# Second feed-forward with four chunk pairs whose weight sums are made in DRAM

## The chip, the cores and the metric

The kernel runs on one core of a Trainium2 chip. The metric is the device time of one execution in microseconds (us); lower is better. A profiled execution also gives a span, from the first to the last instruction of the program, which leaves out what lies around it. Engines are called as the profile calls them: PE (TensorE, matrix multiply), PEld (its weight loads), DVE (VectorE), ACT (ScalarE), POOL (GpSimd) and SP (SyncE, which here only issues transfers).

## The reference, cut to what matters

One layer of an encoder block on 256 positions with 1024 features, all in 32-bit floats:

```python
h = rmsnorm(x, ffn1_pre_g);  x = x + 0.5 * rmsnorm(swiglu(h, ffn1_w_in, ffn1_w_down), ffn1_post_g)
#  mixer: a gated linear recurrence and a forgetting attention on one projection of x, merged by gates
#  cross attention to 256 memory positions
h = rmsnorm(x, ffn2_pre_g);  x = x + 0.5 * rmsnorm(swiglu(h, ffn2_w_in, ffn2_w_down), ffn2_post_g)

def swiglu(h, w_in, w_down):
    gate, up = jnp.split(h @ w_in, 2, axis=-1)      # w_in: 1024 x 5632
    return (jax.nn.silu(gate) * up) @ w_down        # w_down: 2816 x 1024
```

The change is in how the last line of the layer, the second feed-forward, gets `h @ w_in`.

## The kernel before

**Units.** Every weight matrix lies in DRAM as units of 128 x 1024 floats (512 KB). `load_split` (L134) loads one unit into a tile `raw` by a transfer that SP issues (L143), ACT copies it, rounded, to `hi` (L145) and DVE subtracts to get `lo` (L147). Products of two such split operands take three matmuls: hi·hi, hi·lo and lo·hi. There are four `raw` buffers and eight `hi` and eight `lo` buffers. A `raw` buffer is free again when L147 has read it, a `hi`/`lo` pair when its last matmul has. Each call appends its transfer to the list `loads`, and SP issues in that order.

**The feed-forward.** `ffn` (L418) cuts the 2816 hidden columns into 11 chunks of 256. A chunk's weights are four units of `w_in` (two halves of the 1024 inputs by gate and up columns side by side); its share of `w_down` is two units. In the second feed-forward chunks 0 and 1 are done row-wise (`act_tok`), chunks 2, 3, 4, 5 and 8 column-wise (`act_col`, L453), each with 32 matmuls of 512 columns and 32 of 256. `down` (L486) takes a finished chunk through its two units of `w_down`, 12 matmuls of 512 columns for each half of the positions.

**Pairs.** Chunks 6 and 7, and 9 and 10, are done together (`act_pair`, L548), in both feed-forwards (`PAIRS`, L36). The 2 x 2 block product of the two halves of x (positions by inputs) with the two chunks' weights (inputs by chunks) is done with seven block products in place of eight, each of 12 matmuls of 512 columns. For that, four differences of blocks of x are formed once (`pair_inputs`, L506, after chunk 2), and sums of weight blocks are formed for each pair: W00+W01, W01+W11, W00+W01+W11 and the sum of all four. DVE adds them in SBUF (L573) in tiles `sraw` of four further buffers (tag `extra`), so that a pair loads eight units, splits fourteen pairs of tiles and adds eight times. Its activations come out by rows and need eight 128 x 128 transposes (`flush`, L427). Between two block products `step_between` puts one half of a `down`, 12 matmuls.

**Order of the work.** The program is written as one stream; a scheduler orders each engine's instructions by that stream, except where `after(n)` or `issue_after` ties them to a certain matmul or transfer. `row_of` (L348) turns the column of row factors into a row by two small transfers on POOL's queue through DRAM; `act_col` and `pair_inputs` need that row. After the last pair the `down` of chunk 7 follows, and then those of chunks 8 to 10, cut by output columns.

Of the kernel before, what the change touches and what calls it, by code (L numbers as in the profile page):

```python
# [18 lines left out]
P = 128  # L19
D = 1024  # L20
# [12 lines left out]

STAG = 3

PAIRS = {"f1_in": (6, 9), "f2_in": (6, 9)}  # L36

L_ACT = 21
L_F1 = 24
# [41 lines left out]
def block_kernel(ctx: ExitStack, tc: tile.TileContext, wts, head_in, gf_in, x_in, mem_in, memT_in, cols, rows, fbias, masks, out):  # L81
# [48 lines left out]

    place = {}

    def parts_of():
        return [wp.tile([P, D], F32R, tag=t, name=nm(t), bufs=8) for t in ("hi", "lo")]  # L134

    def load_split(src, n=512, behind=None, parts=None):

        raw = wp.tile([P, D], F32, tag="raw", name=nm("raw"), bufs=4)
        hi, lo = parts or parts_of()
        r, h, l = raw, hi, lo  # L140
        if n < 512:
            r, h, l = (p.rearrange("p (k n) -> p k n", k=2)[:, :, :n] for p in (raw, hi, lo))
        loads.append(nc.sync.dma_start(r, src).ins)  # L143
        with tc.issue_after(behind[0]) if behind else nullcontext():
            S.copy(h, r)  # L145
        with tc.issue_after(behind[1]) if behind else nullcontext():
            V.tensor_tensor(out=l, in0=r, in1=h.bitcast(F32), op=ALU.subtract)  # L147
        return hi, lo
# [270 lines left out]
    def ffn(w_in, w_dn, X, r2, n_tok, i_row, first_half, second_half=None):  # L419
# [83 lines left out]

        def pair_inputs():  # L506
            rho = sp.tile([P, P], F32, tag="c1", name=nm("rho"), bufs=7)
# [3 lines left out]
            V.reciprocal(q, r2[1])  # L511
            V.tensor_tensor(out=q, in0=r2[0], in1=q, op=ALU.mult)
            xf = [m4([P, 4, T], n="xf") for _ in range(2)]
            for k in range(2):
                for i in range(2):
                    x = X.t[2 * k + i].bitcast(F32)
                    V.tensor_tensor(out=xf[k][:, 2 * i : 2 * i + 2], in0=x[:, :, 0], in1=x[:, :, 1], op=ALU.add)
                V.tensor_tensor(out=xf[k][:, :, P:], in0=xf[k][:, :, P:], in1=bc(rho, [P, 4, P], 1), op=ALU.mult)
            a, b, d, e = (xf[k][:, :, h * P : h * P + P] for h in range(2) for k in range(2))
            ss = [m4([P, 2, 4, P], n="ss") for _ in range(2)]  # L520
            de, aed, ad, baed = (t[:, i] for t in ss for i in range(2))
            V.tensor_tensor(out=de, in0=d, in1=e, op=ALU.subtract)
            V.tensor_tensor(out=aed, in0=a, in1=de, op=ALU.subtract)
            V.tensor_tensor(out=ad, in0=a, in1=d, op=ALU.subtract)
            V.tensor_tensor(out=baed, in0=b, in1=aed, op=ALU.subtract)
            out = {}
            for n, x in (("baed", baed), ("aed", aed), ("de", de), ("ad", ad), ("e", e)):
                t = m4([P, 2, 4, P], F32R, "sx")
                split(t[:, 0], t[:, 1], x)
                out[n] = t  # L530
            return out, q

        def sum_load(c, n, halves):
            t = []
            for j in range(2):
                r = wp.tile([P, D], F32, tag="extra", name=nm("sraw"), bufs=4)
                more(r, c, *halves[0], j, None)
                t.append(r)
            return t

        def more(r, c, k, n, j, op):
            src = wts[_AT[w_in] + 4 * (c + n) + 2 * k + j - 4]
            if op is None:
                loads.append(nc.sync.dma_start(r, src).ins)
            else:
                G.dma_start(r, src, accum_op=op)

        def act_pair(c, between):  # L548
            sx, q = pairs_in
# [4 lines left out]
            def of_x(k):  # L554
                return lambda kk: (X.hi(4 * k + kk, 0, P), X.lo(4 * k + kk, 0, P))

            def splits(t):
                u = []
                for r in t:
                    p = parts_of()  # L560
                    split(p[0], p[1], r)
                    u.append(p)
                return u

            def raws(k, n):
                t = [wp.tile([P, D], F32, tag="raw", name=nm("raw"), bufs=4) for _ in range(2)]
                for j in range(2):
                    more(t[j], c, k, n, j, None)
                return t

            def add(t, o):
# [14 lines left out]
            def half_tile(n):  # L586
                return sp.tile([P, 512], F32, tag="z2", name=nm(n), bufs=3)

            sums, both = sums_of_pair.pop(c)
# [4 lines left out]
            product(b0, of_x(0), splits(sums), True)  # L594
            S.copy(p1, b0)
            step_between()
# [5 lines left out]
            add(sums, both)  # L602
            add(both, raw)
            b3 = trp()
            product(b3, of("de"), splits(sums), True)
            add(sums, raw)
            step_between()
            b1 = trp()
            product(b1, of("aed"), splits(sums), True)
# [8 lines left out]
            add(sums, raw)  # L618
            step_between()
            b4 = mm()  # L620
            product(b4, of("ad"), splits(both), True)
# [8 lines left out]
            product(b4, of("e"), splits(sums), False)  # L630
            with tc.high_priority():
                t = half_tile("c10")
                V.tensor_tensor(out=t, in0=v, in1=b4, op=ALU.add)
# [4 lines left out]
                step_between()  # L638

        def pair_loads(c):  # L640
            if c in pairs and c not in sums_of_pair:
                with tc.issue_after(loads[-1]):
                    sums_of_pair[c] = sum_load(c, 0, ((0, 0), (0, 1))), sum_load(c, 1, ((0, 1), (1, 1)))

        sums_of_pair = {}
        pairs, pairs_in = PAIRS[w_in], None
        for c in range(n_tok):
            acts[c] = m4([P, 2, 2, T], F32R, "act")
        for h in range(2):
            m = len(log)  # L650
            for c in range(n_tok):
                act_tok(c, h)
            if h == 0 and n_tok:
                second_half(m)
                row = row_of(fac[3])
        accs = None
        done = 0
        if callable(r2):
# [8 lines left out]
        for c in range(n_tok, NFF):  # L667
            if c - 1 in pairs:
                continue
            if c in pairs:  # L670
                pair_loads(c)
            acts[c] = m4([P, 2, 2, T], F32R, "act")
            if c in pairs:
                acts[c + 1] = m4([P, 2, 2, T], F32R, "act")
                downs = [(i, h) for i in range(done, min(c, NFF - STAG - 1)) for h in range(2)]
                done = max(done, min(c, NFF - STAG - 1))
# [7 lines left out]
                act_pair(c, [lambda i=i, h=h: one(i, h) for i, h in downs])  # L684
            elif c == 2 and first_half:
                n = len(log)
                (outs,) = act_first((c,), mm)
                for h in range(2):
                    flush(n + L_ACT + 24 * h)
                    act_evac(outs[h], c, h)  # L690
            else:
# [16 lines left out]
            if c == 2 and pairs:  # L708
# [29 lines left out]

    X1 = Joined()
    heads, raw1 = [], []
    for kb in range(KB):
# [813 lines left out]
```

## Time and profile before

| What | Value |
|---|---|
| median of 3 runs | 776.87 us (776.84 to 778.01) |
| the profiled execution itself | 776.83 us |
| its span | 774.6 us |
| granted PE clock over the span | 0.998 |
| bytes moved by DMA | 148.08 MB, 191 GB/s on the mean |
| transfers of whole units on SP's queue | 231 into `raw`, 16 into `sraw` |

The span is 2.2 us shorter than the execution's own time. Busy times are shares of the span. Matmuls are pipelined, and the length the profile gives one is not the time until the next can start, so in what follows the time of a group of matmuls is read from one start to another.

### The profile page before, as it was taken

To read this page: it belongs to the slowest core of one execution; us is meant where nothing else is said; L and a number is where in the kernel's file an instruction comes from. 1 tells how busy PE (TensorE), PEld (TensorE's weight loads), DVE (VectorE), ACT (ScalarE), POOL (GpSimd) and SP (SyncE) were. 2 spreads that over 40 slices of the span, in tenths; PEclk is the share of its full clock that TensorE was granted. 3 is DMA by queue.
4 is the path that set the end of the run, shared out by engine and by line. 5 is a ranking of instruction groups with operands and counts; after the bars stand their busy time and mean duration, and the time that the engine had idled before them with its cause. 6 is when DMAs were issued, how large, how long until landed. Compare 5 with 4: busy or idle time off the path is not lost.

```text
span 774.6 us, 11943 instructions
## 1 busy us (share of the span) xinstructions
PE 766.7 (99%) x4454; PEld 654.9 (85%) x4454; DVE 636.3 (82%) x989; ACT 489.5 (63%) x807; POOL 15.8 (2%) x39
## 2 busy tenths in 40 slices
PE   9999999999999999999999999999999999999996
PEld 7888888888888998898888888889888888888875
DVE  6797999998778899888776665885579698999993
ACT  7666565768765678557676345863668556565762
POOL 0000000000000101100000000000000000000000
PEclk9999999999999999999999999999999999999999
DMA  9749477255744545834676654465175637467241
GB/s 340 266 140 303 160 260 274 101 194 195 228 160 146 180 144 183 281 110 176 203 265 229 216 176 159 156 201 207 39 247 179 195 119 260 166 226 289 82 136 55
DMA packets 44507, 148.08 MB, mean 191 GB/s; under 512 B 5145, under 2 KB 8865, under 8 KB 44449
## 3 DMA queue, kind: packets, MB, share of 16 engines
q1 hardware_dynamic: 43168, 144.83, 54.3%
q0 software_dynamic: 848, 2.12, 1.1%
q8 instruction: 35, 0.57, 0.3%
q10 hardware_dynamic: 432, 0.37, 0.1%
q14 instruction: 24, 0.19, 0.1%
HBM read 146.24 MB, written 1.06 MB: 190 GB/s over the span
## 4 chain that ended last, share of the span: by engine, by line
PE 89%; DVE 6%; ACT 2%; DMA 1%; issue 1%; DVEq 0%; ACTq 0%; SPq 0%
PE acc L95 38%; PE mm L95 38%; PE tr L95 11%; DVE lo L147 1%; DVE lo L166 1%; DMA raw<-in_wts_dram 1%; PE tr L377 1%; DVE k L970 1%; DVE qf L970 1%; PE tr L436 1%; ACT hi L165 1%; ACT f L1008 0%; PE tr L1194 0%; DVE sraw L573 0%; ACT hi L145 0%
## 5 line engine op out<-in xcount | busy, mean ns | idle before, releaser
L147 DVE TENSOR_TENSOR lo<-raw,hi 128x1024 fp32r<-128x1024 f32 (+1 forms) x220 | 261.1, 1202 | 45.6 <-ACT hi L145 39.3
L145 ACT CAST hi<-raw 128x1024 fp32r<-128x1024 f32 (+1 forms) x220 | 223.8, 1035 | 79.9 <-DMA raw<-in_wts_dram 38.6
L95 PE MATMUL mm<-hi,hlT 128*128 128x512 f32 (+1 forms) x544 | 164.6, 380 | 0.0
L95 PEld LDWEIGHTS mm<-hi,hlT 128*128 128x128 f32 x544 | 100.3, 188 | 16.6
L95 PE MATMUL acc<-hi,act 128*128 128x512 f32 x352 | 113.5, 391 | 0.2 <-ACT act L165 0.2
L95 PE MATMUL mm<-lo,hlT 128*128 128x512 f32 (+1 forms) x272 | 102.0, 380 | 0.0
L95 PEld LDWEIGHTS acc<-hi,act 128*128 128x128 f32 x352 | 66.1, 188 | 14.0 <-ACT act L165 0.6
L95 PE MATMUL acc<-lo,act 128*128 128x512 f32 x176 | 69.2, 393 | 0.0
L95 PE MATMUL acc<-hlT,hi 128*128 128x512 f32 x272 | 68.7, 393 | 0.0
L95 PE MATMUL mm<-hlT,hi 128*128 128x512 f32 (+1 forms) x256 | 60.1, 366 | 0.0
L95 PEld LDWEIGHTS mm<-lo,hlT 128*128 128x128 f32 x272 | 51.0, 188 | 8.4 <-DVE lo L147 0.4
L95 PEld LDWEIGHTS acc<-hlT,hi 128*128 128x128 f32 x272 | 48.9, 189 | 8.7
L165 ACT CAST hi<-sraw 128x1024 fp32r<-128x1024 f32 x40 | 41.5, 1053 | 14.4 <-DVE sraw L573 10.7
L95 PEld LDWEIGHTS mm<-hlT,hi 128*128 128x128 f32 x256 | 44.9, 189 | 6.5
L166 DVE TENSOR_TENSOR lo<-sraw,hi 128x1024 fp32r<-128x1024 f32 x40 | 48.5, 1220 | 0.0
L95 PE MATMUL tr<-hlT,hi 128*128 128x512 f32 x176 | 44.6, 393 | 0.0
L95 PEld LDWEIGHTS acc<-hlT,lo 128*128 128x128 f32 x272 | 37.2, 190 | 2.7
L95 PEld LDWEIGHTS acc<-lo,act 128*128 128x128 f32 x176 | 33.1, 188 | 7.1 <-DVE lo L147 0.7
L95 PE MATMUL acc<-hlT,lo 128*128 128x256 f32 x272 | 38.4, 283 | 0.0
L95 PE MATMUL mm<-hlT,lo 128*128 128x256 f32 x224 | 36.9, 284 | 0.3 <-DVE lo L147 0.3
L95 PEld LDWEIGHTS tr<-hlT,hi 128*128 128x128 f32 x176 | 31.6, 189 | 5.6
L95 PEld LDWEIGHTS mm<-hlT,lo 128*128 128x128 f32 x224 | 32.6, 190 | 2.6 <-DVE lo L147 0.5
(294 smaller groups left out, 1271.9 us busy)
## 6 DMA issues: line engine op xcount, KB each, us to landing
raw<-in_wts_dram SPq DMA_DIRECT2D x231, 512.0 KB, 4.4
sraw<-in_wts_dram SPq DMA_DIRECT2D x16, 512.0 KB, 5.9
raw<-in_gf_dram SPq DMA_DIRECT2D x12, 344.0 KB, 3.8
head<-in_head_dram SPq DMA_DIRECT2D x7, 392.0 KB, 6.7
grow<-in_rows_dram SPq DMA_DIRECT2D x4, 512.0 KB, 5.4
xs<-in_x_dram SPq DMA_DIRECT2D x2, 512.0 KB, 7.8
cbm<-cd POOLq DMA_DIRECT2D x2, 512.0 KB, 8.5
brow<-in_rows_dram SPq DMA_DIRECT2D x4, 256.0 KB, 3.6
```

Source lines behind the costliest of these rows:

```text
L95: log.append(PE.matmul(*args, **kw).ins)
L145: S.copy(h, r)
L147: V.tensor_tensor(out=l, in0=r, in1=h.bitcast(F32), op=ALU.subtract)
L165: a = S.copy(hi, src)
L166: b = V.tensor_tensor(out=lo, in0=src, in1=hi.bitcast(F32), op=ALU.subtract)
L377: PE.transpose(blocks[-1][1], src(kb), ident)
L436: PE.transpose(trv[:, j, h * P : (h + 1) * P], ats[c, h][:, j * P : (j + 1) * P], ident)
L970: V.tensor_tensor(out=tv, in0=tv, in1=other, op=ALU.mult)
```

## The change

The second feed-forward gets four pairs, chunks 3 and 4, 5 and 6, 7 and 8, 9 and 10. Only chunk 2 is left column-wise. The pairs of the first feed-forward keep `act_pair`.

The four weight sums of each pair are made in DRAM. `plan` lists 32 jobs, eight for each pair. A job copies a 512 KB block to a DRAM tile, by a transfer on SP's queue, and then adds another block to it by an accumulating transfer on POOL's queue. `background`, called behind each load of `load_split`, starts one job where the number of loads so far is in `SUMS_AT`. Eight of the jobs of each 16 start from a block of the weights, the other eight from a tile of an earlier job. Load 72 is the first of the mixer and load 204 the first of the second feed-forward; the 32nd job hangs on load 211, the last of chunk 1.

`act_pair_summed` loads all fourteen tiles of a pair, six blocks as they are and eight sums, through `load_split`. It has no additions on DVE and does not use the `sraw` buffers. `pair_inputs` is done ahead of chunk 2 in the stream, and the four additions that join hi and lo of x stand before it, behind the first half of chunks 0 and 1. Of the `down`s, chunk 0 and 1 lie in the first pair, 2 and 3 in the second, 4 and 5 in the third, 6 in the fourth.

```diff
+SUMS_AT = (*range(74, 84, 3), *range(90, 150, 5), *range(151, 230, 4),)
-PAIRS = {"f1_in": (6, 9), "f2_in": (6, 9)}
+PAIRS = {"f1_in": (6, 9), "f2_in": (3, 5, 7, 9)}
...
+    def plan(w_in, cs):
+        first, second, third = [], [], []
+        for c in cs:
+            t = dp.tile([8, P, D + 16], F32, name=nm("sums"))
+            t = sums[w_in, c] = [t[i, :, :D] for i in range(8)]
...
+            for j in range(2):
+                first += [(t[j], b(0, 0, j), b(0, 1, j)), (t[2 + j], b(1, 1, j), b(0, 1, j))]
+                second += [(t[4 + j], t[j], b(1, 1, j))]
+                third += [(t[6 + j], t[4 + j], b(1, 0, j))]
+        jobs.extend(first + second + third)
+
+    def background():
+        at = len(loads)
+        if jobs and at in SUMS_AT:
+            to, x, y = jobs.pop(0)
+            with tc.issue_after(loads[-1]):
+                nc.sync.dma_start(to, x)
+            G.dma_start(to, y, accum_op=ALU.add)
...
         loads.append(nc.sync.dma_start(r, src).ins)
+        background()
...
+        def act_pair_summed(c, between):
...
+            def plain(k, n):
+                return [unit(w_in, 4 * (c + n) + 2 * k + j) for j in range(2)]
+            def summed(i):
+                return [load_split(sums[w_in, c][i + j]) for j in range(2)]
...
+            for i in range(len(late)):
+                flush(n + 26 + 24 * i)
...
+            product(b0, of_x(0), plain(0, 0), True)
+            S.copy(p1, b0)
+            step_between()
+            product(b0, of_x(1), plain(1, 0), False)
...
+            product(b2, of("baed"), plain(1, 1), True)
...
+            product(b3, of("de"), summed(0), True)
+            step_between()
+            product(b1, of("aed"), summed(4), True)
...
+            product(b4, of("ad"), summed(2), True)
...
+            product(b4, of("e"), summed(6), False)
...
+            if c == 2 and not first_half and pairs:
+                pairs_in = pair_inputs()
...
-                downs = [(i, h) for i in range(done, min(c, NFF - STAG - 1)) for h in range(2)]
+                upto = min(c - 1 if c - 2 in pairs or c + 2 in pairs else c, NFF - STAG - 1)
+                downs = [(i, h) for i in range(done, upto) for h in range(2)]
...
+    for i in range(0, len(PAIRS["f2_in"]), 2):
+        plan("f2_in", PAIRS["f2_in"][i : i + 2])
```

More of the change, by code (lines that the diff above doesn't have):

```diff
@@ L531, in pair_inputs, with block, chain_loads @@
             return out, q
-        def sum_load(c, n, halves):
-            t = []
+        def block(r, c, k, n, j):
+            loads.append(nc.sync.dma_start(r, wts[_AT[w_in] + 4 * (c + n) + 2 * k + j - 4]).ins)
+        def chain_loads(c, k, n):
+            t = [wp.tile([P, D], F32, tag="extra", name=nm("sraw"), bufs=4) for _ in range(2)]
             for j in range(2):
-                r = wp.tile([P, D], F32, tag="extra", name=nm("sraw"), bufs=4)
-                more(r, c, *halves[0], j, None)
-                t.append(r)
-            return t
[L541 to L546, printed above, removed]
+                block(t[j], c, k, n, j)
+            return t
         def act_pair(c, between):
@@ L593, in act_pair @@
             b0 = mm()
-            product(b0, of_x(0), splits(sums), True)
+            product(b0, of_x(0), splits(chain), True)
             S.copy(p1, b0)
-            step_between()
+            for _ in range(2 if c == 3 else 1):
+                step_between()
             b2 = trp()
@@ L601, in act_pair @@
             step_between()
-            add(sums, both)
+            add(chain, both)
             add(both, raw)
             b3 = trp()
-            product(b3, of("de"), splits(sums), True)
-            add(sums, raw)
+            product(b3, of("de"), splits(chain), True)
+            add(chain, raw)
             step_between()
             b1 = trp()
-            product(b1, of("aed"), splits(sums), True)
+            product(b1, of("aed"), splits(chain), True)
             with tc.high_priority():
@@ L617, in act_pair @@
                 act_evac(b0, c, 0)
-            add(sums, raw)
+            add(chain, raw)
             step_between()
@@ L655, in ffn @@
                 row = row_of(fac[3])
+                if pairs:
+                    xf = [pair_joined(k) for k in range(2)]
         accs = None
@@ L690, in ffn @@
                     act_evac(outs[h], c, h)
+            elif c in TOKS[w_in]:
+                n = len(log)
+                wait = 24 if c - 2 in pairs else 0
+                for h in range(2):
+                    flush(n + L_ACT + wait + 16 * h)
+                    act_tok(c, h)
             else:
@@ L707, in ffn @@
                 accs = [[acc(), acc()], [acc(), acc()]]
-            if c == 2 and pairs:
+            if c == 2 and first_half and pairs:
+                xf = [pair_joined(k) for k in range(2)]
                 pairs_in = pair_inputs()
```

87 lines of the change are left out of this document (74 added, 13 removed).

## The prediction

> **What bounds the kernel now.** I read the page first, then busy time by windows, the timelines of PE and DVE, and the waits of SP.
>
> ```profile
> span 774.6 us, 11943 instructions
> ...
> PE 766.7 (99%) x4454; PEld 654.9 (85%) x4454; DVE 636.3 (82%) x989; ACT 489.5 (63%) x807; POOL 15.8 (2%) x39
> ...
> PE 89%; DVE 6%; ACT 2%; DMA 1%; issue 1%; DVEq 0%; ACTq 0%; SPq 0%
> ```
>
> PE is busy all the time and carries nine tenths of the chain that ended last. The second feed-forward, where the change is, runs from about 588 us to the end; its column chunks and pairs lie in these windows (window, length, then busy time of PE, PEld, DVE, ACT and POOL with counts, granted clock, share of the DMA engines, GB/s):
>
> ```profile
> 622.00:672.00 50.00, 50.00 (x268) 43.18 (x267) 45.14 (x60) 27.09 (x41) 0.00 (x0) 1.00 0.59 211
> 672.00:708.00 36.00, 36.00 (x164) 29.76 (x163) 33.99 (x36) 25.66 (x31) 0.00 (x0) 1.00 0.64 229
> 720.00:748.00 28.00, 28.00 (x126) 22.85 (x124) 27.97 (x32) 18.93 (x25) 0.00 (x0) 1.00 0.35 114
> ```
>
> PE has no idle time there, though DVE is full (27.97 of 28.00). So nothing PE waits for can be taken away in this stage: only fewer matmuls shorten it, and any new wait lengthens it.
>
> **What the change takes from PE.** Matmuls follow each other without gaps, so a piece costs the distance from its first start to the start of the next piece.
>
> ```profile
> 627.98 1.98 PE L95 MATMUL mm<-hlT,hi 128*128 128x512 f32 x8
> ...
> 639.13 0.40 PE L95 MATMUL acc<-hi,act 128*128 128x512 f32 x1
> ```
> ```profile
> 677.82 0.39 PE L95 MATMUL tr<-hi,sx 128*128 128x512 f32 x1
> ...
> 680.54 0.39 PE L95 MATMUL acc<-hi,act 128*128 128x512 f32 x1
> ```
> ```profile
> 707.75 0.62 PE L436 MATMUL tr<-ident,at 128*128 128x128 f32 x4
> 708.12 0.70 PE L95 MATMUL mm<-hlT,hi 128*128 128x512 f32 x2
> ```
>
> Chunk 3, a column chunk, takes 639.13 - 627.98 = 11.15 us; two take 22.3. One block product takes 680.54 - 677.82 = 2.72 us; a pair has seven, 19.04, and eight transposes at 0.37 us for four, 0.74: 19.8 us. A pair in place of two column chunks saves 2.5 us. Chunks 3, 4, 5 and 8 leave the column form and two pairs come in addition, so PE loses **5.0 us** of work. The `down`s are only moved (a half is 12 matmuls of the same size, 2.72 us).
>
> **What it asks of the loads.** This is the step that decides. A pair before loaded eight units for its fourteen splits and made the rest by additions:
>
> ```profile
> L573 DVE TENSOR_TENSOR sraw<-sraw,raw 128x1024 f32<-128x1024 f32 x24 | 28.8, 1220 | 0.1
> ...
> L573 DVE TENSOR_TENSOR sraw<-sraw,sraw 128x1024 f32<-128x1024 f32 x8 | 9.5, 1218 | 0.0
> ```
>
> The 32 rows are four pairs of eight; the two pairs of this feed-forward lose sixteen additions, 19.5 us of DVE, and PE gains nothing by that, because it did not wait. In exchange every pair loads fourteen tiles, and with the four units of two `down`s 18 pass the four `raw` buffers, while `sraw` lies idle. PE's time for it is 19.8 + 4 x 2.72 = 30.7 us: **one load every 1.70 us**. A column chunk with its `down` took 11.15 + 5.44 us for six loads, one every 2.77. The rate of such a ring is not set by the bytes alone. SP waits for a buffer to come free for more than half of the span, and a load lands after 3.0 us at the least, 4.3 on the median and 10.4 at the most:
>
> ```profile
> SPq L143 <- DVE lo L147: 414.2, 166, 21.9
> ```
> ```profile
> DMA to landing us min/median/max: 3.0/4.3/10.4
> ```
>
> ```profile
> L147 DVE TENSOR_TENSOR lo<-raw,hi 128x1024 fp32r<-128x1024 f32 (+1 forms) x220 | 261.1, 1202 | 45.6 <-ACT hi L145 39.3
> L145 ACT CAST hi<-raw 128x1024 fp32r<-128x1024 f32 (+1 forms) x220 | 223.8, 1035 | 79.9 <-DMA raw<-in_wts_dram 38.6
> ...
> raw<-in_wts_dram SPq DMA_DIRECT2D x231, 512.0 KB, 4.4
> ...
> cbm<-cd POOLq DMA_DIRECT2D x2, 512.0 KB, 8.5
> ```
>
> A turn of a buffer is the issue and landing (4.4 us), the rounding on ACT (1.04) and the subtraction on DVE (1.20), 6.6 us for four loads if nothing stands in between. Two places of DVE's timeline show what it makes. Around 570 us loads are the limit and DVE and ACT have almost nothing else to do:
>
> ```profile
> 568.57 2.35 DVE L147 TENSOR_TENSOR lo<-raw,hi 128x1024 fp32r<-128x1024 f32 x2
> 571.71 1.22 DVE L147 TENSOR_TENSOR lo<-raw,hi 128x1024 fp32r<-128x1024 f32 x1 [0.79 <-ACT hi L145]
> ...
> 578.56 1.23 DVE L147 TENSOR_TENSOR lo<-raw,hi 128x1024 fp32r<-128x1024 f32 x1 [0.68 <-ACT hi L145]
> ```
>
> From the first start to the last there are six further subtractions in 9.99 us (three rows are left out, two of them with the name `w` for `lo`), **1.67 us** a load. In the first feed-forward the same ring runs beside the evacuations of column chunks:
>
> ```profile
> 56.10 2.36 DVE L147 TENSOR_TENSOR lo<-raw,hi 128x1024 fp32r<-128x1024 f32 x2
> ...
> 62.39 1.22 DVE L147 TENSOR_TENSOR lo<-raw,hi 128x1024 fp32r<-128x1024 f32 x1
> 64.15 1.23 DVE L147 TENSOR_TENSOR lo<-raw,hi 128x1024 fp32r<-128x1024 f32 x1 [0.55 <-ACT hi L145]
> 66.25 1.23 DVE L147 TENSOR_TENSOR lo<-raw,hi 128x1024 fp32r<-128x1024 f32 x1 [0.87 <-ACT hi L145]
> 67.39 0.42 DVE L219 TENSOR_TENSOR gate<-mm,plo 128x256 f32<-128x256 f32 x1
> 67.80 1.22 DVE L147 TENSOR_TENSOR lo<-raw,hi 128x1024 fp32r<-128x1024 f32 x1
> 68.94 0.42 DVE L219 TENSOR_TENSOR gate<-mm,plo 128x256 f32<-128x256 f32 x1
> 69.39 0.69 DVE L464 TENSOR_TENSOR gate<-gate,row 128x512 f32<-128x512 f32 x1
> 70.00 1.22 DVE L147 TENSOR_TENSOR lo<-raw,hi 128x1024 fp32r<-128x1024 f32 x1
> 71.13 0.42 DVE L219 TENSOR_TENSOR up<-tr,plo 128x256 f32<-128x256 f32 x1
> 72.71 1.22 DVE L147 TENSOR_TENSOR lo<-raw,hi 128x1024 fp32r<-128x1024 f32 x1 [1.16 <-ACT hi L145]
> ```
>
> From 56.10 to 72.71 there are nine further subtractions, **1.85 us** a load; from 62.39 on five, 2.06. PE was not hurt, because it asked for one every 2.77.
>
> Now the sum, counted from the first matmul of the first pair. The loads to go from there are 4 x 14 for the pairs, 16 for the `down`s 0 to 7 and 6 for 8 to 10: 78. Eight are ahead (four in `hi` and `lo`, four landed), and I take the eighth as split by 6 us: four subtractions and chunk 2's last evacuations. The last is split at 6 + 70 x the time of a load. PE asks for it after 28 products (76.2 us), eight `down`s (43.5), four sets of transposes (3.0) and five steps of three matmuls (0.68 each) into the last `down`s (3.4): 126.1 us. At 1.67 the load is there at 122.9, and nothing is lost. At 1.85 it comes at 135.5, **9.4 us late**. At 2.06 it comes at 150.2, 24.1 late. I take 1.85, because the pairs have small work on DVE and ACT of the kind of that place: five operations of 512 columns, four of 256 and two splits of activations in 30.7 us. It is one lateness that grows through the pairs, not a sum of several.
>
> **The rest of the change.** The accumulating transfer and the copy from DRAM to DRAM do not occur in the trace. The nearest rows are those above for a load, 4.4 us to landing, and for the slowest transfer of this size on POOL's queue, 8.5. They run beside stages that ask for loads at about the pace of a column chunk (four in 11.15 us), and landings of up to 10.4 us left no gap in PE's windows. I take 0 for the 64 transfers. If one pair of them finds a load without lead, it costs 8.5 - 4.4 = 4 us, the upper end; below nothing is excluded, since they take nothing away. On SP each copy is one more issue between loads; SP has 414 us of waiting to put 32 of them in. Copies of the second kind wait for sums started 16 loads or more earlier, 26 us even at 1.67, so the loads queued behind them on SP should not stand. On POOL the accumulations stand ahead of the row's transfers, which `pair_inputs` and chunk 2 need:
>
> ```profile
> 601.69 0.60 POOL L354 DMA_DIRECT2D rd<-runs  x1 [186.01 <-DVE q L511]
> 603.90 0.56 POOL L356 DMA_DIRECT2D row<-rd  x1 [1.61 <-DMA rd<-runs]
> ```
>
> The last job hangs on chunk 1's last load, which is out before the row's first transfer at 601.69, so one accumulation of 8.5 us or so can be in front of it; I count that in the same 0 to 4 us. `pair_inputs` itself moves ahead of chunk 2 on DVE and is not needed before the first pair's third product, which stands behind two products and three halves of `down`s, 5 x 2.72 = 13.6 us. The transposes of a pair's second chunk now come only ten matmuls ahead of the `down` that reads them, twice; ACT's and DVE's split of it could cost half a us each, and lies inside the lateness of the loads.
>
> Sum against the profiled execution's own 776.83 us, which is the median of 776.87 but for 0.04: 776.8 - 5.0 + 9.4 = **781.2 us**. Its span would be 2.2 us less, 779.0.
>
> **The rivals.**
>
> 1. The ring keeps up, and the saving is whole: 776.8 - 5.0 = 771.8 us. It decides by one number. With 1.72 us a load or less nothing is late; at 1.79 lateness equals the saving. For it: 1.67 was held around 570 us, DVE has 19.5 us less to add, and the longest crowd before cost PE nothing. Against it: 1.67 was held only with DVE and ACT nearly free. Bytes would not forbid it: a load every 1.70 us is 524288 / 1.70 = 308 GB/s, over the 229 of the windows above. [...]
>
> 2. The ring is as slow as in the later part of the second stretch, 2.06 us a load, because ACT and DVE run in order and, once PE is late, a copy of its result stands in front of a rounding that could run: 776.8 - 5.0 + 24.1 = 795.9 us. For it: PE's lead is gone early, and those copies then wait. Against it: the last loads of that stretch ran beside four `sraw` loads, which the new pairs don't have.
>
> 3. The jobs crowd out loads ahead of the second feed-forward, 4 us on top of either case: with the saving whole 775.8 us, within 0.2% of before; with the forecast 785. For it: the transfers go through the engines that the loads use. [...]
>
> 4. The change doesn't do what it says: sums not ready when loaded. The last job hangs on load 211, and the third pair's sums are read some 45 loads later, over 75 us. I give it next to nothing.
>
> **How the numbers follow.** The forecast, a ring near 1.85 with lateness of 5.5 to 16 us (777 to 788 us), gets 0.52; rival 1 gets 0.24; rival 2, from 788 up, 0.14; rival 3 on a whole saving, with the part of the forecast that comes out near the old time, 0.10. A measurement of this kernel can tell about 0.2%, 1.6 us, from no change. Faster by more than that are rival 1 and a sliver of the near cases, 0.26; within it 0.11; slower 0.63. Cases of both signs count, so the range goes from the whole saving, 772, to nearly all of rival 2, 795. The forecast's own range is 777 to 788.
>
> **What would show it.** Right: in the four pairs PE gets idle time, ended by DVE `lo` L147, of about 9 us; subtractions of L147 follow each other every 1.8 to 1.9 us there; ACT waits for `raw` loads far longer than before; the DMA share in the pairs rises to some 0.85 (0.64 x 308 / 229) while the 16 additions of L573 are gone. The matmuls of one pair without its waits take 19.8 us. Wrong: no PE idle in the pairs with L147 every 1.7 us (rival 1); PE idle before 600 us, beside accumulating transfers (rival 3); PE waiting for `sx` or for activations in place of weights.

## The result and the profile after

After takes **799.57 us** (median, 796.87 to 805.3), before 777.11 us in the same runs: 1.0291 times as long, 95% interval 1.0265 to 1.0316. The prediction was 781.2 us, range 772 to 795. The direction was right, the size was not. The profiled execution of after took 800.83 us.

The page of after: span, engines, chain of work that ended last, and the issues of transfers with their median us to landing.

```profile
span 799.0 us, 11973 instructions
...
PE 770.8 (96%) x4382; PEld 652.5 (82%) x4382; DVE 632.1 (79%) x979; ACT 500.8 (63%) x811; POOL 42.5 (5%) x71
...
PE 55%; DMA 18%; DVE 15%; ACT 6%; issue 5%; SPq 0%; POOL 0%; DVEq 0%; ACTq 0%; POOLq 0%
...
raw<-in_wts_dram SPq DMA_DIRECT2D x231, 512.0 KB, 5.3
sums<-in_wts_dram POOLq DMA_DIRECT2D x32, 512.0 KB, 8.1
```

The count of matmuls fell by 72, yet the span grew by 24.4 us. PE carried 89% of the chain and DMA 1%; now 55% and 18%. A weight load lands after 5.3 us, 4.4 before; an accumulating transfer (POOLq) after 8.1.

Three matmuls cut the span: the first of the second feed-forward (chunk 0), the first of the first pair, and the last of all. PE's timeline of before, then of after:

```profile
587.81 1.52 PE L95 MATMUL mm<-w,hlT 128*128 128x512 f32 x6
...
767.58 0.39 PE L95 MATMUL acc<-hi,act 128*128 128x512 f32 x1
```
```profile
601.54 1.30 PE L99 MATMUL mm<-w,hlT 128*128 128x512 f32 x5
...
638.06 0.40 PE L99 MATMUL mm<-hi,hlT 128*128 128x512 f32 x1
...
792.05 0.39 PE L99 MATMUL acc<-hi,act 128*128 128x512 f32 x1
```

So **13.7 us** are lost ahead of the second feed-forward, where the change only adds the jobs (587.81 to 601.54), and **10.7 us** inside it (190.5 in place of 179.8). The prediction had 0 and +4.4. Windows inside the pairs (length, then busy time of PE, PEld, DVE, ACT, POOL, the clock, the share of the DMA engines, GB/s) show PE idle, the matmuls short of full clock, and the load rate up:

```profile
640.00:676.00 36.00, 33.38 (x139) 26.86 (x138) 28.11 (x30) 23.26 (x27) 0.00 (x0) 0.95 0.79 268
676.00:712.00 36.00, 33.27 (x143) 26.95 (x142) 27.88 (x30) 22.02 (x27) 0.00 (x0) 0.95 0.85 287
720.00:748.00 28.00, 26.00 (x116) 20.67 (x114) 21.82 (x25) 17.51 (x21) 0.00 (x0) 1.00 0.89 298
```

The longest waits in the pairs of after (us in total, times, longest):

```profile
ACT hi L177 <- DMA raw<-in_wts_dram: 18.7, 25, 1.6
ACT hi L177 <- DMA raw<-sums: 17.6, 22, 1.8
...
PE mm L99 <- DVE c L734: 5.4, 3, 2.7
```

ACT waits for loads, but PE hardly waits for `lo`: it waits for DVE's `c` (L734, the difference that must read a PSUM bank before product `e` may add to it). One such place, on DVE and then on PE:

```profile
700.71 1.23 DVE L179 TENSOR_TENSOR lo<-raw,hi 128x1024 fp32r<-128x1024 f32 x1 [1.44 <-ACT hi L177]
701.85 0.68 DVE L727 TENSOR_TENSOR vw<-pc,tr 128x512 f32<-128x512 f32 x1
703.27 1.22 DVE L179 TENSOR_TENSOR lo<-raw,hi 128x1024 fp32r<-128x1024 f32 x1 [0.74 <-ACT hi L177]
...
706.15 0.68 DVE L734 TENSOR_TENSOR c<-vw,mm 128x512 f32<-128x512 f32 x1
```
```profile
706.88 0.50 PE L99 MATMUL mm<-hi,sx 128*128 128x512 f32 x1 [2.73 <-DVE c L734]
```

Two theories could explain the waits in the pairs. **Ring**: the four `raw` buffers are too slow a ring, as the prediction said, and `c` is late only because subtractions that wait for loads stand ahead of it. **Bank**: the change leaves no `down` between products `ad` and `e`, which add into the same bank, so PE has to wait there until DVE has read it, whatever the loads do. For the 13.7 us there were also two. **Queue**: small work on POOL stands behind accumulating transfers that wait for their copies. **Traffic**: the transfers of the jobs make the loads land late.

### The profile page after: what moved, and what is told of

It reads as the page before. It is cut to its first block, busy times and chain, and to the rows that moved or that the text cites. A ratio compares the mean times of both kernels' runs of the same rounds, so it can differ in the third digit from the quotient of the medians.

```text
span 799.0 us, 11973 instructions
## 1 busy us (share of the span) xinstructions
PE 770.8 (96%) x4382; PEld 652.5 (82%) x4382; DVE 632.1 (79%) x979; ACT 500.8 (63%) x811; POOL 42.5 (5%) x71
## 3 DMA queue, kind: packets, MB, share of 16 engines
q1 hardware_dynamic: 51232, 174.19, 61.2%
q0 software_dynamic: 5456, 18.90, 13.5%
## 4 chain that ended last, share of the span: by engine, by line
PE 55%; DMA 18%; DVE 15%; ACT 6%; issue 5%; SPq 0%; POOL 0%; DVEq 0%; ACTq 0%; POOLq 0%
PE acc L99 24%; PE mm L99 24%; DMA raw<-in_wts_dram 12%; DVE lo L179 6%; PE tr L99 5%; ACT hi L177 3%; DMA raw<-sums 3%; DVE lo L198 2%; DMA sums<-sums 1%; DMA raw<-in_gf_dram 1%; DMA row<-rd 1%; DVE act L198 1%; DVE k L1094 0%; PE tr L468 0%; DMA head<-in_head_dram 0%
## 5 line engine op out<-in xcount | busy, mean ns | idle before, releaser
L179 DVE TENSOR_TENSOR lo<-raw,hi 128x1024 fp32r<-128x1024 f32 (+1 forms) x260 | 309.4, 1204 | 59.1 <-ACT hi L177 55.1
L177 ACT CAST hi<-raw 128x1024 fp32r<-128x1024 f32 (+1 forms) x260 | 266.4, 1039 | 129.7 <-DMA raw<-in_wts_dram 76.8
L99 PE MATMUL mm<-hi,hlT 128*128 128x512 f32 (+1 forms) x576 | 175.6, 381 | 0.0
L162 POOL DMA_DIRECT2D sums<-in_wts_dram x32 | 26.5, 828 | 510.0 <-DMA sums<-in_wts_dram 297.2
L99 PE MATMUL tr<-hi,sx 128*128 128x512 f32 x144 | 46.7, 389 | 0.0
L99 PE MATMUL mm<-hlT,hi 128*128 128x512 f32 (+1 forms) x192 | 44.3, 357 | 1.5 <-DVE at L476 1.5
L99 PE MATMUL mm<-hi,sx 128*128 128x512 f32 x96 | 34.3, 420 | 5.5 <-DVE c L734 5.4
L99 PEld LDWEIGHTS mm<-hlT,hi 128*128 128x128 f32 x192 | 33.2, 189 | 5.9 <-DVE at L476 1.7
L99 PEld LDWEIGHTS tr<-hi,sx 128*128 128x128 f32 x144 | 27.0, 188 | 5.6
L99 PE MATMUL tr<-hlT,hi 128*128 128x512 f32 x112 | 28.2, 392 | 0.0
```

The lines of the kernel that those rows point to most:

```text
L99: log.append(PE.matmul(*args, **kw).ins)
L162: G.dma_start(to, y, accum_op=ALU.add)
```

## The experiments

Times are medians; each ratio is to before, run beside it (776.3 to 777.4 us), with its 95% interval.

### The two losses apart

After without the jobs:

```diff
-            t = dp.tile([8, P, D + 16], F32, name=nm("sums"))
-            t = sums[w_in, c] = [t[i, :, :D] for i in range(8)]
+            t = sums[w_in, c] = [wts[_AT[w_in] + 4 * c + i - 4] for i in range(8)]
...
-        jobs.extend(first + second + third)
```

> After without the 32 background jobs: plan lists none, and the eight sums of a pair are read from plain blocks of w_in in place of the DRAM tiles, so the second feed-forward multiplies by the wrong weights; all loads, roundings and products stay. Theory A (the jobs cost about 15.5 us ahead of the first pair, by holding POOL's queue and the DMA engines; the pairs cost the rest, 13.6 - 5.0): 784 us, 782 to 787, with the second feed-forward starting where it did before. Rival (what the prediction said: jobs 0 to 4 us, the loss is in the pairs): 796 us or more.

786.59 us, ratio 1.0122 (1.0099 to 1.0146), in Theory A's range. The same three matmuls in it:

```profile
588.19 1.07 PE L99 MATMUL mm<-w,hlT 128*128 128x512 f32 x4
...
624.53 0.40 PE L99 MATMUL mm<-hi,hlT 128*128 128x512 f32 x1
...
777.62 0.39 PE L99 MATMUL acc<-hi,act 128*128 128x512 f32 x1
```

The second feed-forward starts 0.4 us later than in before, and loses 9.7 us inside, nearly as much as in after.

Jobs only, in before, with `plan` and `background` as in after; nobody reads the sums:

```diff
         loads.append(nc.sync.dma_start(r, src).ins)
+        background()
...
+    for i in (3, 7):
+        plan("f2_in", (i, i + 2))
     X1 = Joined()
```

> Before, with the same 32 jobs at the same loads and nobody reading the sums (the pairs stay as they were; the output is not touched). Theory A: 777 + 12 to 16 = 789 to 793 us. Rival (jobs cost 0 to 4 us by themselves): 777 to 781 us.

787.89 us, ratio 1.0145 (1.0124 to 1.0167), 1.1 us under Theory A's range and far over the rival's. So there are two separate causes: 9.5 us without the jobs and 10.8 with the jobs alone. Together they make 20.3 of after's 22.5 us; the other 2.2 come with both, or lie in the spread of after's executions (796.87 to 805.3).

### What a job costs

Copies only, from the kernel with the jobs alone:

```diff
-            G.dma_start(to, y, accum_op=ALU.add)
```

> As the kernel with the jobs alone, but the accumulating transfers left out: 32 copies on SP's queue, POOL's queue as before; the sums, which nobody reads, are then single blocks. If the loss is POOL's in-order queue (small work of the mixer standing behind an accumulating transfer that waits for its copy): 777 to 779 us. If it is the traffic on the DMA engines: the copies move two of the five blocks of a job, so about 0.4 of the loss, 782 to 784 us.

779.08 us, ratio 1.0019 (1.0002 to 1.0036). This is about what the queue theory gave, and less than traffic in proportion would cost. Two copies on SP's queue for each job, nothing on POOL's:

```diff
...
-            G.dma_start(to, y, accum_op=ALU.add)
+            with tc.issue_after(loads[-1]):
+                nc.sync.dma_start(spare[len(jobs) % 4], y)
```

> Before with 32 jobs, each of two plain copies on SP's queue (the second to a spare DRAM tile) in place of a copy and an accumulating transfer; nobody reads either. Four of the five blocks of a job's traffic stay, POOL's queue is as before. If the traffic costs in proportion: 784 to 786 us. If POOL's queue or the accumulating transfer itself does: 779 to 781 us.

783.37 us, ratio 1.0103 (1.0062 to 1.0144): more than the 779 to 781 of a cost that sits on POOL alone, though nothing was added to POOL, and just under the range for traffic. Its executions lie apart: three took 782.7 to 784.0 us and one 789.6, and the profile is of that one. In it the second feed-forward starts at 600.39 us, with the jobs alone at 600.61; by their pages both kernels move the same, 181.64 and 181.65 MB. SP's queue is hardly the cause: the profile shows no wait of SP at a copy, and the issue of one took 0.5 to 0.6 us.

The jobs again, with the accumulations put one job later in the stream:

```diff
-            G.dma_start(to, y, accum_op=ALU.add)
+            last.append((to, y))
+            if len(last) > 1 or not jobs:
+                G.dma_start(*last.pop(0), accum_op=ALU.add)
...
```

> Before with the 32 jobs unused, but each accumulating transfer is put on POOL's queue where the next job's copy starts, so that its copy has landed before POOL comes to it; the traffic is the same. If the loss is POOL's queue, in which the mixer's small work stands behind an accumulating transfer that waits for its copy: 779 to 781 us. If it is the traffic: 786 to 788 us, as with the jobs unchanged.

790.14 us, ratio 1.017 (1.0146 to 1.0194). This run does not separate the two theories, because the scheduler gave POOL the same order as without the edit. What makes PE wait is better read from the chain of waits of the kernel with the jobs alone, around PE's longest stop in the mixer:

```profile
330.96 11.88 DMA raw<-in_wts_dram
342.89 0.93 issue
343.82 0.69 ACT junk L313 x2
...
347.26 0.76 DVE G L1162
349.35 0.67 PE acc L97 x4
```

A weight load lands 11.9 us after its issue, ACT's rounding of it stands at the head of ACT's queue, the small sum of squares `junk` behind it is late, then DVE's `G`, then PE. POOL is not in this chain. After has the same at the same place (a load of 12.66 us, PE idle for 4.84), and so has the kernel with two copies (a load of 8.44 us, PE idle for 2.3). And the landing of the loads grows with the traffic. These are the loads of `load_split` issued between 165 and 600 us, where the jobs run: before, copies only, two copies, jobs alone, after:

```profile
DMA to landing us min/median/max: 3.0/4.2/9.0
```
```profile
DMA to landing us min/median/max: 3.1/4.4/9.7
```
```profile
DMA to landing us min/median/max: 3.1/4.9/9.3
```
```profile
DMA to landing us min/median/max: 3.0/5.5/11.9
```
```profile
DMA to landing us min/median/max: 3.1/5.8/12.7
```

Of some 117 weight loads in that stretch 3, 2, 6, 13 and 21 took over 8 us. The four profiled executions with added transfers lost 2.9, 12.8, 12.7 and 24.0 us against that of before (the 24.0 are after's, with the loss in the pairs). So the landing shows that loads come later, but not by itself what that costs.

The five blocks of a job in the expectations are the author's count. The pages count one read and one written for a copy (16.8 MB each for the 32, against before) and two and two for a whole job, with the accumulating transfer as with two copies (33.6 MB each); no run shows a fifth.

The queue alone does not explain the loss: 6.2 of the 10.8 us come with nothing added to POOL, and at PE's longest stop a late load is what it waits for in the end. So at least that part is traffic. The other 4.5 us, between two kernels that move the same bytes by the profile's count, are open: POOL's queue, something of the accumulating transfer itself, or the spread between executions.

Other places for the jobs:

```diff
-SUMS_AT = (*range(74, 84, 3), *range(90, 150, 5), *range(151, 230, 4),)
+SUMS_AT = (*range(16, 60, 3), *range(64, 84, 3), 104, 109, 114, *range(164, 212, 4),)
```

> Before with the 32 jobs unused, as before it, but started behind other loads: 14 in the first feed-forward, 7 in the first third of the mixer, 12 behind loads 164 to 208; none behind loads 85 to 103 and 115 to 163, the stretches in which the lateness of PE grew with the jobs. The traffic is the same in sum. If what a job costs depends on what stands beside it: 777 to 780 us. If each job costs about a third of a us wherever it is: 786 to 789 us.

800.63 us, ratio 1.03 (1.0262 to 1.0339), outside both ranges: the jobs cost more than twice as much as before the move. 14 of them had gone to the first feed-forward, where none had been before. There, between 60 and 140 us, loads now land after up to 14.6 us (10.3 before).

### What the pairs cost

Bank against ring: the `down`s moved (edit of `act_pair_summed`).

```diff
             product(b0, of_x(0), plain(0, 0), True)
-            step_between()
...
-            step_between()
             b2 = trp()
...
-            step_between()
+            if len(between) > 3:
+                step_between()
             b3 = trp()
...
-            step_between()
+            if len(between) > 1:
+                step_between()
             b4 = mm()
```

> After, with the halves of the downs moved: none behind the first two products of a pair, one behind each of the last ones ahead of e, so that 12 matmuls stand between the product ad and the product e on the same bank. Theory B (PE waits in the pairs for DVE's c11, which must read the bank before e may add to it, and DVE gets to it late because its queue stands at subtractions that wait for loads): the gaps of 2.4 and 2.9 us and the slow matmuls behind them go, 799.6 - 6 = 793 us, 790 to 796. Rival (the loads come too slowly, as the prediction said; the wait moves to the next product): 799 to 801 us.

799.22 us, ratio 1.0298 (1.0248 to 1.0347): unchanged, as the rival said. The wait only moves, to copies and transposes:

```profile
PE tr L468 <- DVE at L476: 4.0, 4, 1.5
PE mm L99 <- ACT pc L711: 2.3, 2, 1.2
PE mm L99 <- DVE c L734: 2.1, 2, 1.4
```

So the bank is not the cause. Eight buffers in the kernel without jobs:

```diff
-        raw = wp.tile([P, D], F32, tag="raw", name=nm("raw"), bufs=4)
+        tag = "extra" if wide and len(loads) % 2 else "raw"
+        raw = wp.tile([P, D], F32, tag=tag, name=nm("raw"), bufs=4)
...
         def act_pair_summed(c, between):
             sx, q = pairs_in
+            wide.append(c)
```

> The kernel without the jobs (wrong weights in place of the sums, as there), and from the first pair of the second feed-forward on every second load goes to a buffer of the tag extra, so that eight buffers take the loads in turn in place of four. If the turn of the four buffers limits the pairs (the prediction's step): the 13.6 us of waiting after 637 us go nearly all, 786.6 - 8 to 13 = 774 to 779 us. If the rounding on ACT and the subtraction on DVE limit it, or the rate at which transfers land at all: 785 to 788 us, with ACT's wait for raw no shorter in the second case.

779.62 us, ratio 1.0035 (1.002 to 1.005), just over the ring's 774 to 779. Its three matmuls, and a window of its pairs:

```profile
588.69 1.07 PE L99 MATMUL mm<-w,hlT 128*128 128x512 f32 x4
...
631.04 0.40 PE L99 MATMUL mm<-hi,hlT 128*128 128x512 f32 x1
...
771.06 0.39 PE L99 MATMUL acc<-hi,act 128*128 128x512 f32 x1
```
```profile
676.00:712.00 36.00, 36.00 (x164) 29.64 (x164) 29.48 (x33) 24.62 (x29) 0.00 (x0) 1.00 0.88 323
```

From the first pair's first matmul to the last, 140.0 us, 153.1 with four buffers and 154.0 in after; PE is never idle, and the wait for `c` is gone with nothing done about the bank. So the ring of four buffers is shown to be the cause. The rate itself, from DVE's timeline without jobs, four buffers and then eight:

```profile
626.27 1.21 DVE L177 TENSOR_TENSOR lo<-raw,hi 128x1024 fp32r<-128x1024 f32 x1
...
761.46 2.36 DVE L177 TENSOR_TENSOR lo<-raw,hi 128x1024 fp32r<-128x1024 f32 x2 [0.25 <-ACT hi L175]
```
```profile
632.04 1.21 DVE L179 TENSOR_TENSOR lo<-raw,hi 128x1024 fp32r<-128x1024 f32 x1
...
753.14 1.22 DVE L179 TENSOR_TENSOR lo<-raw,hi 128x1024 fp32r<-128x1024 f32 x1
```

Each kernel has 74 such subtractions in its pairs. 72 steps in 135.19 us are **1.88 us** a load; 73 in 121.10 are 1.66, PE's own pace.

### What eight buffers cost

The pairs gain 13.1 us, the kernel only 7.0. The stretch ahead of the first pair is 6 us longer (42.4 in place of 36.3). `rho`, the first operation of `pair_inputs` on DVE, waits for the row of row factors, and the reading of chunk 1's bank (its evacuation) stands behind it; PE waits 4.90 us for that bank, 1.4 with four buffers, and its clock is 0.50 afterwards (619 to 623 us). POOL's two transfers of that row, four buffers and then eight, both without jobs:

```profile
604.13 0.60 POOL L384 DMA_DIRECT2D rd<-runs  x1 [187.99 <-DVE runs L382]
607.10 0.57 POOL L386 DMA_DIRECT2D row<-rd  x1 [2.36 <-DMA rd<-runs]
```
```profile
604.62 0.60 POOL L386 DMA_DIRECT2D rd<-runs  x1 [188.22 <-DVE runs L384]
611.52 0.57 POOL L388 DMA_DIRECT2D row<-rd  x1 [6.30 <-DMA rd<-runs]
```

The first moves 1 KB, and the second waits 6.3 us for it (2.4 with four buffers), beside loads of 512 KB that SP now issues eight deep. Three edits tried to take the row's lateness off PE's path, all on the kernel without jobs and with eight buffers. First, `pair_inputs` behind chunk 2 in the stream:

```diff
-            if c == 2 and not first_half and pairs:
-                pairs_in = pair_inputs()
...
-            if c == 2 and first_half and pairs:
-                xf = [pair_joined(k) for k in range(2)]
+            if c == 2 and pairs:
+                if first_half:
+                    xf = [pair_joined(k) for k in range(2)]
                 pairs_in = pair_inputs()
```

> The kernel without jobs and with eight raw buffers (wrong weights in place of the sums, as there), and pair_inputs put back behind chunk 2 in the stream, so that rho's wait for the row no longer stands on DVE ahead of chunk 1's last evacuation, whose bank chunk 2 needs. If the 5.1 us that PE waits for that evacuation at 614 us are what is left of the pairs' cost: 779.6 - 5 = 774.6 us, 773 to 776, below before. If the wait only moves on (chunk 2 needs the row too): 778 to 780 us.

779.55 us, ratio 1.0042 (1.003 to 1.0054), in the second range: the scheduler left `rho` ahead of the evacuation, and PE waited 4.74 us as before. Second, `rho` tied behind it:

```diff
...
-            V.reciprocal(rho, row[:, :P])
+            with tc.issue_after(at_last[-1]):
+                V.reciprocal(rho, row[:, :P])
```

> The kernel without jobs and with eight raw buffers (wrong weights in place of the sums, as there), and rho's reciprocal tied behind chunk 1's last evacuation on DVE; pair_inputs stays where after has it. (Putting pair_inputs behind chunk 2 in the stream had left rho ahead of that evacuation in DVE's order.) If the 5 us that PE waits for the evacuation at 613 us are the last of the pairs' cost: 779.6 - 5 = 774.6 us, 773 to 776. If chunk 2 then waits for the row in its own place: 778 to 780 us.

779.0 us, ratio 1.0024 (1.0009 to 1.0039): that wait is gone, and PE waits for ACT's copy of `p1` in the first pair, behind the splits of the differences. Third, those splits tied behind that copy:

```diff
...
-            S.copy(p1, b0)
+            with tc.issue_after(S.copy(p1, b0).ins):
+                while x_late:
+                    split(*x_late.pop(0))
```

> The kernel without jobs, with eight raw buffers and rho held (wrong weights in place of the sums, as there); the five splits of the differences of x are tied behind the first pair's copy of p1, so that they no longer stand on ACT ahead of the copies and roundings that the first pair needs. If the last 5 us of the pairs are the chain row, rho, differences, splits, which two in-order engines put ahead of what PE asks for: 779.0 - 4 to 5 = 774 to 775 us, below before. If PE then waits for the splits themselves in the third product: 777 to 780 us.

778.41 us, ratio 1.0027 (1.0013 to 1.004). A wait of PE stays. ACT is idle for 4.36 us before chunk 2's `gate`, and five roundings and the copy of `p1` (`pc`, L717), for which PE waits, come behind it. DVE's part of that `gate` needs the row and comes at 626.91 us, behind `rho` (619.16) and the differences made from it:

```profile
627.62 0.63 ACT L498 ACTIVATE gate<-gate 128x512 f32<-128x512 f32 x1 [4.36 <-DVE gate L497]
```
```profile
634.30 0.79 PE L99 MATMUL mm<-hi,hlT 128*128 128x512 f32 x1 [4.34 <-ACT pc L717]
```

With chunk 2 the only column chunk, there is little other work to cover the row. A kernel that goes to eight buffers only once the row has landed was not run, so that the row's lateness is the whole of these 5 us is argued and not shown.

### Together, and in other ways

Jobs lagged and eight buffers:

> After with both: the accumulating transfers put one job later, and eight buffers for the loads of the four pairs. If POOL's queue and the turn of the four buffers are the two causes: 799.6 - 8 - 10 = 780 us, 775 to 784. If neither is: 796 to 800 us.

789.03 us, ratio 1.0164 (1.0133 to 1.0194), between the two ranges. It is 10.5 us less than after; as the later place of the accumulations brought nothing above, that is put down to the eight buffers. Jobs moved, eight buffers, `pair_inputs` behind:

> After with three edits: the jobs moved as in the kernel that moves them, eight raw buffers in the four pairs, pair_inputs behind chunk 2. All sums are made and read. If the three costs are the ones found and add up: 774.6 + 0 to 3 = 775 to 778 us, about before or a little below. If the jobs cost the same wherever they are: 784 us or more.

800.58 us, ratio 1.0315 (1.029 to 1.0339): the moved jobs cost here what they cost alone, and the second feed-forward starts at 608.00 us, 20.2 later than in before. Eight buffers, `rho` held, and the jobs in stretches that had stayed free:

```diff
...
+SUMS_AT = (74, 77, 80, 83, 104, 108, 112, 116, *range(144, 213, 3), 215)
```

> After with eight raw buffers, rho held, and the jobs behind loads 74 to 83, 104 to 116 and 144 to 215 only, every third load in the last stretch: the stretches in which PE's lateness did not grow with jobs in any kernel so far. All sums are made and read. If jobs cost nothing where loads have slack: 775 to 778 us. If there are too many of them for these stretches (a job each 8 us there in place of one each 11): 779 to 786 us.

799.55 us, ratio 1.0293 (1.0277 to 1.031), over both ranges and 20.5 us over the same kernel without jobs: these stretches had been free only with the few jobs that stood in them. Two pairs from DRAM, two by additions on DVE:

```diff
-    for i in range(0, len(PAIRS["f2_in"]), 2):
-        plan("f2_in", PAIRS["f2_in"][i : i + 2])
+    plan("f2_in", PAIRS["f2_in"][::2])
```

> Four pairs, of which only the first and third take their sums from DRAM (16 jobs, behind loads 74 to 82, 104 to 114 and 164 on); the second and fourth add on DVE as in before. Eight raw buffers from the third product of a summed pair on, rho held. If the cost of the sums in DRAM is the jobs' traffic in places without slack, and DVE has room for every other pair's eight additions: 777 - 5 + 0 to 3 = 772 to 775 us. If DVE, full in the pairs of before, becomes the limit: 777 us or more.

789.74 us, ratio 1.0156 (1.0124 to 1.0189): 16 jobs still put the second feed-forward 8.5 us later (596.30 us), and inside it 4.0 us are lost. After with eight buffers, `rho` held, the splits behind:

> After with eight raw buffers, rho held and the splits behind p1's copy; the jobs where after has them. All sums are made and read. If what is left is the jobs alone: the time of the kernel without jobs plus 11 to 13 us, 785 to 788 us. If jobs and pairs still disturb each other: over 790 us.

791.99 us, ratio 1.0178 (1.0138 to 1.0217), 13.6 over the same without jobs. That is in the range of jobs and pairs that disturb each other, but the traces do not show that: from its first matmul to its last the second feed-forward takes 181.1 us, 181.8 without jobs, and it starts 10.5 us later. So the jobs ahead of it are most of what is left. No DRAM sums at all (the calls of `plan` left out), four pairs adding on DVE:

> After without sums in DRAM: all four pairs load eight units and add on DVE as the two pairs of before did. DVE then has 18 subtractions, 8 additions and some 5 us of small work for a pair with its downs, 36.5 us against PE's 30.7. If DVE's work is the limit: 777 - 5 + 15 to 23 = 787 to 795 us. If the saving is whole: 772 us.

801.85 us, ratio 1.032 (1.0304 to 1.0335). DVE is the limit, and by more than the 787 to 795 expected: the second feed-forward takes 204.9 us, and between 660 and 750 us DVE is busy 87.1 of 90 us and PE 81.0. The same additions on POOL:

```diff
-                    V.tensor_tensor(out=x, in0=x, in1=y, op=ALU.add)
+                    G.tensor_tensor(out=x, in0=x, in1=y, op=ALU.add)
```

> As the kernel with all four pairs adding in SBUF, but the 48 additions of the two feed-forwards are POOL's. No trace has such an addition; POOL's affine_select of 128x512 took 0.63 us, so for 128x1024 with two inputs 1.3 to 2.5 us is an estimate. At 2.5 us the eight of a pair are 20 us beside PE's 30.7, and DVE has 26.7: 773 to 780 us. If an addition takes over 3.8 us, or slows DVE, POOL or DVE is the limit: over 790 us.

850.28 us, ratio 1.0948 (1.0929 to 1.0966). Its groups, POOL's addition and DVE's subtraction (busy, mean ns):

```profile
L602 POOL TENSOR_TENSOR sraw<-sraw,raw 128x1024 f32<-128x1024 f32 x36 | 111.6, 3111 | 64.9 <-DVE lo L198 48.0 <-ACT pc L627 10.1 <-ACT hi L177 4.8
```
```profile
L198 DVE TENSOR_TENSOR lo<-raw,hi 128x1024 fp32r<-128x1024 f32 x24 | 59.2, 2490 | 3.7 <-PE tr L99 3.0 <-ACT hi L197 0.7
```

An addition takes 3.11 us, and this group of 24 subtractions takes 2.49 us each in place of 1.22 in the kernel that adds on DVE. So with the additions on POOL these subtractions of DVE took twice as long, the case for which over 790 us were expected. No version beat before.

## Why the prediction was wrong, step by step

1. **PE's work, -5.0 us: right, by what is left over.** Inside the feed-forward after loses 10.7 us, of which 14.0 (154.0 - 140.0) are the ring and 1.5 PE's wait for the bank behind `rho`; that leaves -4.8.
2. **The ring, +9.4 us: right mechanism and rate, size too small.** 1.88 us a load were measured without jobs, 1.85 were taken. It cost 13.1 us without jobs and 14.0 with them. Of the 3.7 us missing without jobs, 70 loads x 0.03 are 2.1; the rest is the start: the eighth load was split about 7.5 us after the first matmul of the pairs, where 6 were assumed.
3. **How it would show: half wrong.** PE was to be idle for about 9 us and to wait for `lo`. It was idle for 8.4 us from the first pair on, and ACT waited for loads, but most of PE's idle time was ended by `c`, behind the late subtractions in DVE's queue. The engine that ends a wait need not be its cause: mending the bank moved the wait and changed nothing.
4. **The transfers, "I take 0 for the 64 transfers": the step that failed.** They cost 13.7 us in after and 10.8 alone. The argument was that landings of up to 10.4 us had left no gap in PE's windows, so that one slow load could cost 4 us at most. But the landings of over 10 us in before lie in the two feed-forwards (at 70 and 651 us); between 165 and 600 us, where most of the jobs run, the longest was 9.0. There the jobs made many loads late (over 8 us 3 times in before, 13 with the jobs alone, 21 in after), and at the place shown the late load held small work on ACT that PE needed soon. Rival 3 named the mechanism (the pages count SP's and POOL's queues as shares of the same 16 engines, 54.3% and 1.1% in before, 61.2% and 13.5% in after), with a price for one event and not for 32 jobs. Its sign came: between 160 and 590 us PE is busy for 420.8 us, 429.7 in before.
5. **`pair_inputs` not needed early: half wrong.** Its products had cover; the reading of chunk 1's bank behind `rho` on DVE had not (1.5 us).
6. **Rivals 1 and 2:** the ring did not keep up at four buffers (786.6 without jobs); 2.06 us a load was not reached (1.89 in after). Bytes indeed did not forbid 308 GB/s: a slice of before's page has 340, and the window of the pairs with eight buffers 323. That rival 2's 795.9 us lie nearest to the measured time is luck. Rival 4, sums not ready, is not seen.

Without the jobs the forecast would have been 5.4 us short (786.6 against 781.2); the jobs of step 4 bring the other 13.0 of the 18.4.

## What to carry to other kernels

That PE has no gap and SP has time did not make background transfers free (10.8 us with the jobs alone). Look at the landing of every load beside them, in the stage where they will run and not in another, and look for small work that stands behind a load's consumer in an engine's queue. The ring of four buffers could be priced from the profile (1.85 us a load in a crowded stretch, 1.88 measured), and eight mended it (1.66, 13.1 us less in the pairs), but deeper prefetch came with a later landing of a small transfer that other work needed (waited for 6.3 us in place of 2.4). When a wait names an engine, look at what stood ahead in that engine's queue before mending the wait.

## What was not expected of the hardware

After PE's idle of 4.3 us in the kernel with the splits behind, the clock was halved for the next 5 us (windows, the clock is the third last column):

```profile
620.00:627.00 7.00, 7.00 (x41) 6.13 (x40) 6.96 (x14) 2.02 (x3) 0.00 (x0) 1.00 0.20 75
...
636.00:638.00 2.00, 2.00 (x6) 1.52 (x6) 2.00 (x4) 1.54 (x3) 0.00 (x0) 0.50 0.79 274
...
642.00:646.00 4.00, 4.00 (x20) 3.30 (x19) 4.00 (x4) 3.07 (x5) 0.00 (x0) 1.00 0.73 214
```

Twelve matmuls took 5.29 us there (634.30 to 639.59) in place of 2.72, so the stop cost 2.6 us more than its own length. The same followed two stops of 0.48 and 2.14 us in after, with one matmul between them:

```profile
667.00:670.00 3.00, 0.57 (x2) 0.19 (x1) 2.79 (x4) 1.87 (x2) 0.00 (x0) 1.00 0.93 309
...
672.00:673.00 1.00, 1.00 (x4) 0.77 (x3) 1.00 (x2) 0.64 (x1) 0.00 (x0) 0.50 0.78 287
```

In this second case only one matmul ran in 3.1 us. The single stop of 2.73 us shown above was followed by 0.50 too (709 to 711 us), and after one of 2.38 us with `rho` held matmuls start 0.43 us apart in place of 0.23. The wait of 1.4 us for chunk 1's bank, without jobs and with four buffers, left the clock at 1.00 (615 to 620 us). How short a stop is enough, these runs do not show.
